# The low parts of split weights made by an adding DMA instead of vector subtractions

## The chip, the cores and the metric

The kernel runs on one core of one Trainium2 chip. The metric is device microseconds (us) of one execution; the median of several runs counts. The core has five engines with a queue each: TensorE (PE; PEld is its weight load), VectorE (DVE), ScalarE (ACT), GpSimd (POOL) and SyncE (SP, which issues transfers). All of them share 16 DMA engines.

## What is computed

Two layers of an encoder trunk over 512 positions of width 1024, all in float32. Each layer has a mixer (one input projection, a gated part, attention with 8 query and 2 key heads, one output projection) and a channel mixer (up projection, a convolution of width 3 over positions, gate, down projection).

```python
D_MODEL, SEQ, DEPTH, D_FF = 1024, 512, 2, 2816
for i in range(DEPTH):
    h = rms_norm(x, attn_norm_g[i])
    proj = h @ w_in[i]
    q, k, v, u, vv = jnp.split(proj, split_at, axis=-1)
    q = axial_rope(rms_norm(q, q_norm_g[i]), tables)
    k = axial_rope(rms_norm(k, k_norm_g[i]), tables)
    attn_o = gqa_attention(q, k, v)
    sg_o = spatial_gating(jax.nn.gelu(u), jax.nn.gelu(vv),
                          sg_norm_g[i], sg_w[i], sg_b[i])
    merged = jnp.concatenate([rms_norm(attn_o, attn_out_g[i]),
                              rms_norm(sg_o, sg_out_g[i])], axis=-1)
    x = x + merged @ w_o[i]
    h = rms_norm(x, ffn_norm_g[i]) @ w_up[i]
    h = depthwise_conv(h, conv_w[i], conv_b[i])
    gate, up = jnp.split(h, 2, axis=-1)
    x = x + (jax.nn.silu(gate) * up) @ w_down[i]
```

## The kernel before

Matmuls run on a rounded type (float32r). To keep accuracy each operand is split into a rounded high part and a low part, the difference; a product is three matmuls, high x high, high x low, low x high (`mm3`, L258).

All weights lie in memory as a list of 178 chunks of 128 x 1024 values (512 KB), in the order of use: per layer four chunks for vv, four for a1 (keys, values and the first half of the queries), four for u, two for a2 (the other queries), one for ws (the gating weights), four for so and four for ao (the output projection), and then 66 for the up and down projections (`up`, `dn`). The class `WStream` (L86) carries them: `load_to` issues a load from SP into one of 4 raw buffers (`wraw`), `split_to` makes the two parts in one of 6 split buffers (`wspl`, high part in `t[:, 0]`, low part in `t[:, 1]`). The high part is a rounding copy on ACT (L123). The low part is a subtraction, raw minus high (L125), on POOL for u, a2, so and ao (in two halves) and on DVE for all others. A raw buffer comes free when its low part is made, a split buffer when its last matmul has run. `next` (L134) is called where a chunk is used; it asks for loads six chunks ahead and for splits three ahead, and a scheduler then places each instruction in its engine's queue, so that the splits of a chunk stand further ahead where a buffer allows it.

One layer runs like this. `in_group("vv")` and `in_group("a1")` project; between them and beside them DVE makes the row scale r (`row_rsqrt`, `rsqrt`, L210: a chain of a dozen operations on 128 x 4 values), ACT and DVE the gelu and norm of vv (`vv_stat`, `vv_norm`; POOL multiplies vvg by the gain at L409), then the query and key statistics (`qk_stat`, ACT square at L326; `qk_norm`) and the rotation (`rope_pair`, L349 to L355, on DVE for K, on POOL for one pair of queries). At the start of each layer POOL makes the rotary tables (`tab`, L293, L297). A list written by hand, `PROG_AT`, sets the order of the rest of the mixer on TensorE: U are pieces of the u projection, K the transposes of the rotated K (L361), C scores, T transposes of P (L489), Z the output projection. In `up(j)` TensorE multiplies two chunks into two banks, and `up_post` does the convolution and gate on DVE and ACT (L669 to L683). `down(g)` uses pairs of chunks in the same way. DVE's L708 adds to x.

Of the kernel before, what the change touches and what calls it, by code (L numbers as in the profile page):

```python
# [10 lines left out]
F32 = mybir.dt.float32  # L11
F32R = mybir.dt.float32r
I32 = mybir.dt.int32
AF = mybir.ActivationFunctionType
ALU = mybir.AluOpType
# [70 lines left out]
class WStream:  # L86
# [25 lines left out]
    def split_to(self, n):  # L112
        nc = self.nc
        while self.split < min(n, len(PLAN)):
            i = self.split
            key, n_el = PLAN[i]
            raw = self.raw.pop(i)
            t = self.split_pool.tile([P, 2, CH], F32R, name="wspl")
            pieces = 2 if i == 0 or pool_lo(key) else 1
            st = n_el // pieces  # L120
            for a in range(0, n_el, st):
                e = slice(a, a + st)
                nc.scalar.activation(out=t[:, 0, e], in_=raw[:, e], func=AF.Copy)  # L123
                lo = nc.gpsimd if pool_lo(key) else nc.vector
                lo.tensor_tensor(out=t[:, 1, e], in0=raw[:, e], in1=t[:, 0, e].bitcast(F32), op=ALU.subtract)  # L125
            self.spl[i] = t
            self.split += 1
# [11 lines left out]
        return self.spl.pop(i)  # L139


def pool_lo(key):
    return key[0] in POOL_LO


ROPE_ENG = (0, 0)
WARM = 8
POOL_LO = ("u", "a2", "so", "ao")


@with_exitstack
# [661 lines left out]
```

## Time and profile before

| | |
|---|---|
| runs | 1126.06 us median of 3 (1125.95 to 1127.46) |
| span of the profiled execution | 1123.4 us; its own time is not listed apart from the span, which is 2.7 us under the median of the runs |
| mean granted TensorE clock | 0.989 |
| PE, DVE, ACT, POOL busy | 97%, 71%, 45%, 20% |
| DMA | 99.76 MB, 89 GB/s in the mean |

A row of the waits tells which engine and line waited, for which engine and line, how long in total, how often, and the longest. A timeline row tells the start, the duration, the engine, the line, the operation, output and inputs; idle time before it and what ended that stand in brackets. A window row tells how long each engine was busy in a stretch, the granted clock as a share of full speed, the DMA engines' busy share and GB/s.

### The profile page before, as it was taken

What the parts mean: (1) busy time and instruction counts of PE and PEld (TensorE: products, weight loads), DVE (VectorE), ACT (ScalarE), POOL (GpSimd) and SP (SyncE); (2) the same over time, 40 slices, a digit from 0 to 9 for tenths busy, and PEclk for the clock granted to TensorE, in tenths of its full rate; (3) what the DMA queues carried; (4) which work ended last, traced back from release to release, by engine and by line L of the source; (5) the groups of instructions that cost most, each with busy time, mean ns of one, the idle gap of its engine ahead of it and who ended that gap; (6) DMA issues with size and microseconds to landing.
All of it is one profiled execution on the core that took longest, in us unless ns stands there. A gap on an engine that the chain in (4) does not pass through costs nothing.

```text
span 1123.4 us, 13306 instructions
## 1 busy us (share of the span) xinstructions
PE 1085.4 (97%) x5024; PEld 903.1 (80%) x5024; DVE 801.9 (71%) x1210; ACT 502.2 (45%) x786; POOL 224.0 (20%) x221
## 2 busy tenths in 40 slices
PE   9969899999999999999999789999999999999998
PEld 7859687788888888888888688787888888888887
DVE  7898998787753777347668899977877447763573
ACT  6348683454431444224344586644444124441330
POOL 6665642200000000000166564421000000000000
PEclk9989999999999999999999899999999999999999
DMA  7321103232323323232332220122232322323201
GB/s 263 121 94 57 38 1 111 77 106 82 113 89 99 96 92 113 76 111 94 97 114 74 76 76 1 38 75 95 94 113 79 109 94 94 107 81 113 88 25 75
DMA packets 29439, 99.76 MB, mean 89 GB/s; under 512 B 3392, under 2 KB 4032, under 8 KB 29376
## 3 DMA queue, kind: packets, MB, share of 16 engines
q1 hardware_dynamic: 29088, 98.79, 26.3%
q8 instruction: 39, 0.64, 0.2%
q14 instruction: 24, 0.20, 0.1%
q10 hardware_dynamic: 288, 0.14, 0.0%
HBM read 96.82 MB, written 2.10 MB: 88 GB/s over the span
## 4 chain that ended last, share of the span: by engine, by line
PE 71%; DVE 7%; ACT 1%; issue 1%; POOL 1%; DVEq 0%; ACTq 0%
PE dn L261 7%; PE dn L260 7%; PE dn L259 7%; PE upg L260 7%; PE upg L261 7%; PE upv L261 7%; PE upv L259 7%; PE upv L260 7%; PE upg L259 7%; PE pT L489 1%; DVE wspl L125 1%; DVE xl L255 1%; PE vv L260 1%; PE vv L259 1%; PE vv L261 1%
## 5 line engine op out<-in xcount | busy, mean ns | idle before, releaser
L123 ACT ACTIVATE wspl<-wraw 128x1024 fp32r<-128x1024 f32 (+1 forms) x207 | 191.8, 938 | 249.9 <-PE dn L261 136.7
L125 DVE TENSOR_TENSOR wspl<-wraw,wspl 128x1024 fp32r<-128x1024 f32 (+1 forms) x151 | 191.4, 1269 | 92.7 <-ACT wspl L123 92.5
L259 PE MATMUL upg<-xh,wspl 128*128 128x512 f32 x352 | 137.4, 390 | 2.1 <-ACT xh L254 2.1
L260 PE MATMUL upg<-xl,wspl 128*128 128x512 f32 x352 | 137.2, 390 | 1.1 <-DVE xl L255 1.1
L261 PE MATMUL upv<-xh,wspl 128*128 128x512 f32 x352 | 137.0, 389 | 0.0
L260 PE MATMUL upv<-xl,wspl 128*128 128x512 f32 x352 | 137.0, 389 | 0.0
L261 PE MATMUL upg<-xh,wspl 128*128 128x512 f32 x352 | 137.0, 389 | 0.0
L259 PE MATMUL upv<-xh,wspl 128*128 128x512 f32 x352 | 136.9, 389 | 0.0
L259 PE MATMUL dn<-g,wspl 128*128 128x512 f32 x352 | 136.9, 389 | 0.0
L260 PE MATMUL dn<-g,wspl 128*128 128x512 f32 x352 | 136.9, 389 | 0.0
L261 PE MATMUL dn<-g,wspl 128*128 128x512 f32 x352 | 136.9, 389 | 0.0
L671 ACT ACTIVATE ht<-ht,pk_sb 128x512 f32<-128x512 f32 x88 | 70.9, 808 | 69.0 <-DVE ht L669 69.0
L708 DVE TENSOR_TENSOR x<-x,dn 128x512 f32<-128x512 f32 x63 | 43.0, 685 | 66.3 <-PE dn L261 66.2
L672 DVE SCALAR_TENSOR_TENSOR ht<-ht,pk_sb 128x511 f32<-128x511 f32 x88 | 65.7, 747 | 33.0 <-ACT ht L671 33.0
L125 POOL TENSOR_TENSOR wspl<-wraw,wspl 128x512 fp32r<-128x512 f32 x56 | 77.6, 1408 | 49.8 <-ACT wspl L123 49.8
L259 PEld LDWEIGHTS upg<-xh,wspl 128*128 128x128 f32 x352 | 66.1, 188 | 16.5 <-ACT xh L254 2.9
L260 PEld LDWEIGHTS upg<-xl,wspl 128*128 128x128 f32 x352 | 66.1, 188 | 15.6 <-DVE xl L255 2.1
L682 ACT ACTIVATE g<-ht 128x512 fp32r<-128x512 f32 x44 | 27.7, 631 | 110.8 <-DVE ht L678 110.8
L261 PEld LDWEIGHTS upv<-xh,wspl 128*128 128x128 f32 x352 | 66.1, 188 | 13.8
L259 PEld LDWEIGHTS upv<-xh,wspl 128*128 128x128 f32 x352 | 66.1, 188 | 13.7
L259 PEld LDWEIGHTS dn<-g,wspl 128*128 128x128 f32 x352 | 66.1, 188 | 13.7
L260 PEld LDWEIGHTS dn<-g,wspl 128*128 128x128 f32 x352 | 66.1, 188 | 13.7
(198 smaller groups left out, 2049.5 us busy)
## 6 DMA issues: line engine op xcount, KB each, us to landing
wraw<-in_wts SPq DMA_DIRECT2D x177, 512.0 KB, 3.4
x<-in_xT SPq DMA_DIRECT2D x8, 256.0 KB, 6.0
out_y<-x SPq DMA_DIRECT2D x7, 256.0 KB, 2.0
wraw<-in_wts SPq DMA_DIRECT2D x2, 256.0 KB, 3.9
sgn<-in_gq SPq DMA_DIRECT2D x2, 256.0 KB, 4.7
rope<-in_rope SPq DMA_DIRECT2D x2, 256.0 KB, 4.9
pk_sb<-in_pk SPq DMA_DIRECT2D x1, 208.0 KB, 7.2
gq_sb<-in_gq SPq DMA_DIRECT2D x2, 64.0 KB, 5.1
```

The lines of the kernel that those rows point to most:

```text
L123: nc.scalar.activation(out=t[:, 0, e], in_=raw[:, e], func=AF.Copy)
L125: lo.tensor_tensor(out=t[:, 1, e], in0=raw[:, e], in1=t[:, 0, e].bitcast(F32), op=ALU.subtract)
L255: V.scalar_tensor_tensor(out=lo, in0=x_sb[d], scalar=gcol, in1=hi.bitcast(F32), op0=ALU.mult, op1=ALU.subtract)
L259: T.matmul(out, lhsT=lh, rhs=rh, start=start, stop=False)
L260: T.matmul(out, lhsT=lh, rhs=rl, start=False, stop=False)
L261: T.matmul(out, lhsT=ll, rhs=rh, start=False, stop=stop)
L489: T.transpose(bank[:, b * P:(b + 1) * P], pt[b][:, s * P:(s + 1) * P], ident)
L671: A.activation(out=tt, in_=h, func=AF.Identity, scale=col(PK_CW + 2 * NCT + ct), bias=col(PK_CB + ct))
L672: V.scalar_tensor_tensor(out=tt[:, 1:S], in0=h[:, 0:S - 1], scalar=col(PK_CW + ct), in1=tt[:, 1:S], op0=ALU.mult, op1=ALU.add)
L682: A.activation(out=hi, in_=t[0], func=AF.Copy)
L708: V.tensor_tensor(out=x_sb[dt], in0=x_sb[dt], in1=bank, op=ALU.add)
```

## The change

The low part of every chunk but those of vv is made in three steps: ACT writes the high part, ACT writes the negated high part into the place of the low part, and a DMA issued from POOL adds the raw chunk onto it. The vv chunks keep the subtraction on DVE. The halves on POOL go with the subtractions there, so all chunks but the first are split in one piece. There are 170 such DMAs of 512 KB each, and 170 more copies on ACT; 142 subtractions leave DVE and 56 (halves) leave POOL. One line is added above the rest, so the line numbers after it are higher by one.

```diff
-            pieces = 2 if i == 0 or pool_lo(key) else 1
+            pieces = 2 if i == 0 else 1
             st = n_el // pieces
             for a in range(0, n_el, st):
                 e = slice(a, a + st)
                 nc.scalar.activation(out=t[:, 0, e], in_=raw[:, e], func=AF.Copy)
-                lo = nc.gpsimd if pool_lo(key) else nc.vector
+                if key[0] in DMA_LO:
+                    nc.scalar.activation(out=t[:, 1, e], in_=raw[:, e], func=AF.Copy, scale=-1.0)
+                    nc.gpsimd.dma_start(out=t[:, 1, e].bitcast(F32), in_=raw[:, e], accum_op=ALU.add)
+                    continue
+                lo = nc.gpsimd if key[0] in POOL_LO else nc.vector
                 lo.tensor_tensor(out=t[:, 1, e], in0=raw[:, e], in1=t[:, 0, e].bitcast(F32), op=ALU.subtract)
...
-def pool_lo(key):
-    return key[0] in POOL_LO
...
-POOL_LO = ("u", "a2", "so", "ao")
+POOL_LO = ()
+DMA_LO = ("a1", "u", "a2", "ws", "so", "ao", "up", "dn")
```

POOL's queue in the first layer, from the last sums of squares to the vvg products and the rotation of a pair of queries. Before:

```order
L226 TENSOR_TENSOR sqacc<-sqacc,sq 128x512 x2
L293 TENSOR_TENSOR tab<-rope,gq_sb 128x256
L297 TENSOR_TENSOR tab<-rope,gq_sb 128x4x16 x4
L293 TENSOR_TENSOR tab<-rope,gq_sb 128x256
L297 TENSOR_TENSOR tab<-rope,gq_sb 128x4x16 x4
L125 TENSOR_TENSOR wspl<-wraw,wspl 128x512 x6
L409 TENSOR_TENSOR vvg<-vvg,sgn 128x512 x2
L125 TENSOR_TENSOR wspl<-wraw,wspl 128x512
L409 TENSOR_TENSOR vvg<-vvg,sgn 128x512 x2
L125 TENSOR_TENSOR wspl<-wraw,wspl 128x512 x5
L349 TENSOR_TENSOR rot<-qn,tab 128x512
```

The same place of POOL's queue now:

```order
L227 TENSOR_TENSOR sqacc<-sqacc,sq 128x512 x2
L126 DMA wspl<-wraw 128x1024
L294 TENSOR_TENSOR tab<-rope,gq_sb 128x256
L298 TENSOR_TENSOR tab<-rope,gq_sb 128x4x16 x4
L294 TENSOR_TENSOR tab<-rope,gq_sb 128x256
L298 TENSOR_TENSOR tab<-rope,gq_sb 128x4x16 x4
L126 DMA wspl<-wraw 128x1024 x6
L410 TENSOR_TENSOR vvg<-vvg,sgn 128x512 x4
L126 DMA wspl<-wraw 128x1024 x3
L350 TENSOR_TENSOR rot<-qn,tab 128x512
```

The first a1 chunk's low part is issued ahead of the tables; those of the three other a1 chunks and of the first three u chunks stand between the tables and vvg; the four vvg products now stand together.

ACT's queue in the steady part of the up projection, one block of `up` (L671 and L672 are the convolution's middle tap, L677 and L678 the silu, L682 and L683 the rounded gate product). Before:

```order
L671 ACTIVATE ht<-ht,pk_sb 128x512
L123 ACTIVATE wspl<-wraw 128x1024
L677 ACTIVATE ht<-ht 128x512
L123 ACTIVATE wspl<-wraw 128x1024
L671 ACTIVATE ht<-ht,pk_sb 128x512
L682 ACTIVATE g<-ht 128x512
```

The same block of ACT's queue now, where L123 is the rounded and L125 the negated copy:

```order
L672 ACTIVATE ht<-ht,pk_sb 128x512
L123 ACTIVATE wspl<-wraw 128x1024
L678 ACTIVATE ht<-ht 128x512
L125 ACTIVATE wspl<-wraw 128x1024
L123 ACTIVATE wspl<-wraw 128x1024
L672 ACTIVATE ht<-ht,pk_sb 128x512
L125 ACTIVATE wspl<-wraw 128x1024
L683 ACTIVATE g<-ht 128x512
```

The rounded copies stand where they stood; each negated copy follows one instruction later.

## Rows read from the trace of the kernel before

**Rows 1.** The page, part 1: busy us (share of the span) and instructions.

```profile
PE 1085.4 (97%) x5024; PEld 903.1 (80%) x5024; DVE 801.9 (71%) x1210; ACT 502.2 (45%) x786; POOL 224.0 (20%) x221
```

**Rows 2.** Waits of PE and PEld over the span.

```profile
PE tr L361 <- DVE rot L355: 17.1, 2, 9.4
PE pT L489 <- DVE att L505: 4.9, 2, 2.5
PE ps L231 <- DVE asq L524: 4.1, 2, 2.0
PE pT L489 <- ACT p L470: 2.7, 2, 1.4
...
PEld pT L489 <- POOL wspl L125: 3.5, 2, 1.8
```

**Rows 3.** Windows: each engine's busy us (instructions), granted clock, DMA share, GB/s.

```profile
300.00:350.00 50.00, 50.00 (x223) 41.38 (x222) 25.94 (x30) 14.96 (x17) 0.00 (x0) 1.00 0.30 96
...
8.00:12.00 4.00, 4.00 (x13) 3.12 (x13) 3.08 (x4) 4.00 (x7) 2.65 (x2) 1.00 1.03 407
...
72.00:76.00 4.00, 1.58 (x6) 1.51 (x7) 4.00 (x7) 0.46 (x1) 3.40 (x2) 0.50 0.00 0
...
628.00:632.00 4.00, 3.96 (x13) 3.30 (x14) 4.00 (x6) 1.11 (x2) 2.67 (x2) 0.51 0.05 5
```

**Rows 4.** Timeline of ACT in the up projection: a split and its wait.

```profile
299.82 1.06 ACT L123 ACTIVATE wspl<-wraw 128x1024 fp32r<-128x1024 f32 x1 [0.82 <-PE upv L261]
```

**Rows 5.** The page, part 5: groups, busy us, mean ns of one, idle before.

```profile
L123 ACT ACTIVATE wspl<-wraw 128x1024 fp32r<-128x1024 f32 (+1 forms) x207 | 191.8, 938 | 249.9 <-PE dn L261 136.7
L125 DVE TENSOR_TENSOR wspl<-wraw,wspl 128x1024 fp32r<-128x1024 f32 (+1 forms) x151 | 191.4, 1269 | 92.7 <-ACT wspl L123 92.5
...
L125 POOL TENSOR_TENSOR wspl<-wraw,wspl 128x512 fp32r<-128x512 f32 x56 | 77.6, 1408 | 49.8 <-ACT wspl L123 49.8
```

**Rows 6.** Load queue from 240 to 560 us (packets, MB, share); loads, ns; landing.

```profile
q1 hardware_dynamic: 8643, 31.01, 29.4%
...
L108 SPq DMA_DIRECT2D wraw<-in_wts x177: 327/328/665, 3.5 to 1067.8; - x177
...
DMA to landing us min/median/max: 3.1/3.4/7.4
```

**Rows 7.** Timelines of DVE and POOL in the first layer, and DVE in the second.

```profile
31.25 1.17 DVE L214 TENSOR_SCALAR rxr<-rxt 128x4 int32<-128x4 int32 x1
...
36.60 0.16 DVE L218 SCALAR_TENSOR_TENSOR rxr<-rxa,rxr 128x4 f32<-128x4 f32 x1
...
61.31 1.21 DVE L332 TENSOR_SCALAR qass<-qass 128x24 f32<-128x24 f32 x1
...
29.99 1.15 POOL L297 TENSOR_TENSOR tab<-rope,gq_sb 128x64 f32<-128x64 f32 x4
31.10 5.05 POOL L125 TENSOR_TENSOR wspl<-wraw,wspl 128x512 fp32r<-128x512 f32 x4
...
48.12 3.37 POOL L409 TENSOR_TENSOR vvg<-vvg,sgn 128x512 f32<-128x512 f32 x2 [3.10 <-DVE vvg L407]
...
587.53 1.21 DVE L214 TENSOR_SCALAR rxr<-rxt 128x4 int32<-128x4 int32 x1
```

**Rows 8.** Timelines of ACT and PE around the query statistics and the K wait.

```profile
58.19 1.61 ACT L326 ACTIVATE sq<-a 128x384 f32<-128x384 f32 x4
...
612.39 1.61 ACT L326 ACTIVATE sq<-a 128x384 f32<-128x384 f32 x4
...
30.68 0.49 PE L259 MATMUL a<-wspl,xh 128*128 128x512 f32 x1
...
52.58 0.39 PE L259 MATMUL u<-wspl,xh 128*128 128x512 f32 x1
...
607.93 0.39 PE L259 MATMUL u<-wspl,xh 128*128 128x512 f32 x1
...
76.16 0.63 PE L261 MATMUL u<-wspl,xl 128*128 128x512 f32 x1
76.59 0.63 PE L259 MATMUL u<-wspl,xh 128*128 128x512 f32 x1
```

## The prediction

> **What bounds the kernel now.** I read the busy shares first, then the waits of TensorE, then windows. PE is busy 1085.4 of 1123.4 us [rows 1]; whatever the change does elsewhere, it can give back at most the 38 us in which PE stands still, plus what a lowered clock costs, and it can take much more than that by making PE wait for weights. The waits of PE [rows 2] say where those 38 us lie: 17.1 us are two waits (one in each layer) of the K transposes for the rotated K, 4.9 + 2.7 us are waits of the P transposes, 4.1 us the wait for asq. None of any size is for a weight chunk. The windows [rows 3] add two things. From 300 to 350 us, in the up and down projections, PE has no gap at all: 223 matmuls in 50 us, 0.224 us each, so a chunk of 1024 columns (24 matmuls) lasts 5.4 us. And right after the K waits the granted clock stands near 0.5 (0.50 and 0.51, the 1.2 GHz level) before it returns to 1.00. So the kernel has two kinds of stage: a long one (2 x 66 chunks) where weights must come every 5.4 us and nothing can be gained, and the mixer of each layer, where VectorE's chain to K is what PE waits for.
>
> **Up and down projections: the DMA engines.** Here the change must not make weights late. Two numbers decide: how early a chunk is split, and whether the 16 DMA engines can carry it. For the first, the splits of ScalarE [rows 4] wait for the end of a matmul that frees one of six split buffers, so the new chunk is wanted six chunks after the one that was just used up: five lie between, 5 x 5.4 = 27 us, less 2.7 us because the two chunks of a pair are used in alternation. That leaves 24 us. Before, the split took 1.06 + 1.27 us [rows 5]. Now it takes 1.06 for the rounded part, 1.06 for the negated part, an issue on POOL and a transfer. ScalarE's order keeps the rounded part at the same place in each block, the negated one one step later. No row shows a DMA issued from POOL. Its issue lies between 0.33 us (SP's issue of the same 512 KB) and 2.8 us (the two POOL subtractions of a chunk that go away, 1.4 us each) [rows 5, 6]; I take 1 us, nearer to the SP row as both only issue. Landing takes 3.1 us at the least for a plain chunk, 7.4 at the most [rows 6]; with twice the reading I take 6 to 10. Sum 2.1 + 1 + 10 = 13 of 24 us: hidden. A raw buffer, of which there are four, is now held until the transfer lands: load 3.4 to 7.4, split 2.1, issue 1, transfer 6 to 10, so 13 to 20 us of the 4 x 5.4 = 21.7 that four buffers give. Hidden too, with little left at the upper end. ScalarE's added 170 x 1.06 = 180 us lie in its idle time: it is busy 502 us (45%) [rows 1] and goes to about 61%. VectorE loses 142 subtractions of 1.27 us, 180 us, all of it cover for nothing: worth zero in this stage.
>
> For the second: from 240 to 560 us the load queue takes 29.4% of the engines while 59 chunks land [rows 6], so one load costs 0.294 x 320 / 59 = 1.6 us of all 16 engines. An add reads 512 KB twice and writes it once. At the least it costs as much as one load, 1.6 us; the rows give no upper end, so I set it at four loads, 6.4 us, as an assumption. I take two loads, 3.2 us, since the 8:12 window [rows 3] shows the engines moving 407 GB/s when pushed (two readings of 512 KB at that rate are 2.6 us, just under it). Then a chunk needs 1.6 + 3.2 = 4.8 of 5.4 us: 88% busy, but not the bound. This term is zero, and it is the thinnest one: it holds up to 2.4 loads per add.
>
> The Trainium skill speaks to both sides. "Collectives: The Full Stack", section "The bandwidth ceiling", says that an add inside a DMA costs no time of its own but two source reads, which halves the rate; by it the add would be two loads, the same 4.8 us. "DMA: Bandwidth & Descriptors", section "Issuing engines are not separate DMA queues", speaks against the change: transfers issued from POOL share the 16 engines with those from SP, so the added 89 MB are not free. No row here shows either.
>
> **The mixer: what VectorE gains.** In the first layer VectorE's tiny operations take 1.2 us instead of 0.16 while POOL subtracts [rows 7]: four in the chain of r (31.25 to 36.2), two at 43, three from 60.7 to 63.8. Together 4.1 + 1.8 + 2.4 = 8.3 us. The second layer shows the same at the same places, 6.7 us over seven operations, one of the first 1.21 [rows 7]. These POOL subtractions go: 14 chunks per layer, two halves each. Not all of this reaches K. The square of the query projection on ScalarE (58.19, behind a split and the vh copies, which wait for POOL) could start when a1 ends on PE at 52.6; in the second layer 612.39 against 607.9 [rows 8]. So the ceiling is 5.5 + 2.4 = 7.9 of the 9.4 us wait, and 4.5 + 1.9 = 6.4 of the 7.7.
>
> What works against it in the first layer: the low part of a1's second chunk is now issued on POOL behind the rotary tables, which end at 31.1 [rows 7] and a little later now, because the first chunk's issue stands ahead of them. Ready at 32.2 + 1 + 3.4 to 7 = 36.6 to 40.2; PE wants it at 30.7 + 5.4 = 36.1. That stall of 0.5 to 4 us moves the end of a1 with it. On POOL the vvg products of the first layer also stand behind six such issues, the last of which waits for a load that waits for an earlier low part; by my count vvg starts at 48.5 instead of 48.1 [rows 7], but then runs without a subtraction in between. I take 4.5 us for the first layer (0 to 7.9) and 5.5 for the second (2 to 6.4), where the tables are not in the way.
>
> The clock: after the K waits the matmuls start 0.43 us apart [rows 8] instead of 0.224 for some ten instructions, about 2.3 us in each layer. With a wait of 2 to 4 us left it may fall or not; I take half, 2.5 of 4.6 us. The P transposes: 3.5 us of weight loads there wait behind a POOL subtraction [rows 2], and the chain of the second query group runs beside four more. Of 7.6 us of PE waits I take 2 back (0 to 5). Against all that stand some four extra 1.06 us copies per layer on ScalarE while it is nearly full with the softmax: 1 us (0 to 5). In the output projection and at the start of up the low parts leave VectorE and go behind POOL's sums of squares; they are wanted at least 10 us later, so zero.
>
> Whether a DMA issue on POOL holds VectorE as a subtraction does is in no row. "SBUF — State Buffer", section "Who interferes with whom", gives the hold to a VectorE operation with two SBUF inputs beside a POOL instruction that reads SBUF; an issue only writes descriptors, and by it the sum stands. If it held VectorE all the same, this part would be zero.
>
> **Sum.** 4.5 + 5.5 + 2.5 + 2 - 1 = 13.5 us off the span of 1123.4, so 1109.9. The median of the runs, 1126.06, is 2.7 us above the span; carried over, 1112.6: I say 1113, with 1101 (all ceilings: 7.9 + 6.4 + 4.6 + 5 = 24) to 1122 for this case.
>
> **Rivals.**
> *The DMA engines become the bound* (slower). Place: both projections, 132 chunks. Point: an add of more than 2.4 loads (3.8 us). Price: (1.6 + add - 5.4) x 132, less the 13 won elsewhere. At 2.7 loads 5.9 us a chunk, +63, about 1170; at three loads 6.4 us, +127, about 1240; at four, +340, about 1450. For it: adds mean read, read, write through engines that are 29% busy already, and no row bounds the add. Against: 407 GB/s in the start window.
> *POOL's queue turns the mixer around* (slower). 19 issues per layer take the place of 28 subtractions of 1.4 us; at more than 2 us an issue, POOL is busier than before, and vvg, the rotary products and the softmax scaling stand behind issues that wait for ScalarE. At 4 us an issue I count 10 to 20 us lost over both layers: 1128 to 1146.
> *Nothing moves* (no change): the end of a1 and of vvg are held by late low parts, or an issue holds VectorE as the subtraction did. The K waits stay: 1122 to 1129.
> That the subtractions stay where they were can be left out; the program has 170 such DMAs and nine subtractions of vv.
>
> **How the numbers follow.** Forecast 0.55, DMA engines 0.24, POOL's queue 0.10, nothing 0.11. About 0.2% (2.3 us) is what a measurement can tell from no change. Faster: 0.55 and a little of the last, 0.57. Same: 0.09. Slower: 0.34. For 8 in 10 the range runs from 1101 to 1170: above it lies about two thirds of the DMA case, 0.16, and below it 0.03.
>
> **What would show it.** Right: PE without gaps from 250 to 550, DMA share there near 0.9 and landing of the adds under 10 us, VectorE's tiny operations at 0.16 to 0.19 us outside POOL's own products, the K waits down to 2 to 5 us. Wrong: TensorE waiting for wspl by a DMA in the up and down projections with the DMA share at 1, POOL's queue full, or K waits as long as before with vvg later.

## The result, and the profile after

The changed kernel takes 1096.37 us (median of 4 runs, 1094.58 to 1098.38) against 1126.57 us (1125.95 to 1127.46) for the kernel before beside it: a ratio of 0.972, 95% interval 0.9694 to 0.9746. It is 30 us faster where 13 were forecast, and 5 us below the range of 1101 to 1170. The profiled execution of after has a span of 1095.3 us and took 1097.05 us; the span was 1123.4 before, so the traces have 28.1 of the 30 us to explain. Line numbers of after are one higher than before from the split on; L125 is now the negated copy, L126 the adding DMA, and L129 the subtraction of vv.

The page of after, busy us of each engine, then the group of the adding DMA's issues (x count | busy us, mean ns | idle before, releaser):

```profile
PE 1079.0 (99%) x5024; PEld 898.0 (82%) x5024; DVE 597.2 (55%) x1068; ACT 656.9 (60%) x928; POOL 280.0 (26%) x335
...
L126 POOL DMA_DIRECT2D wspl<-wraw x170 | 147.3, 868 | 666.9 <-ACT wspl L125 381.9
```

Against [rows 1], VectorE has lost 205 us of work and ScalarE has gained 155. Neither number is the gain. PE's standing time went from 38.0 to 16.3 us, and that is where 22 of the 28 us are; the other 6 are PE's own busy time (1085.4 to 1079.0), which is shorter where the granted clock no longer falls (4.5 us by the table and the windows below; what made up the rest is open).

The waits of PE in after (us in total, times, longest), to hold against [rows 2]:

```profile
PE tr L362 <- DVE rot L356: 5.8, 2, 5.1
PE pT L490 <- ACT p L471: 1.9, 2, 1.0
PE a L260 <- ACT p L471: 1.4, 2, 0.7
```

The K wait fell from 17.1 to 5.8 us, nearly all of it in the first layer. The wait of the P transposes for att (4.9 us), the wait for asq (4.1 us) and the weight loads behind a POOL subtraction (3.5 us) are no longer in the list. One wait is new: the a2 matmuls (tile a) for ScalarE's p, 0.7 us in each layer.

**Where the 28 us lie.** The same instruction of TensorE in both traces, by its start (us from the start of the span), gives the lead of after at ten points. Of matmuls in three products the first product is taken:

| instruction of PE | before | after | lead | gained since the row above |
|---|---|---|---|---|
| first K transpose, layer 1 | 74.42 | 70.39 | 4.0 | 4.0 |
| first so matmul, layer 1 | 129.7 | 123.8 | 5.9 | 1.9, P transposes |
| first ao matmul, layer 1 | 175.9 | 167.6 | 8.2 | 2.3, output projection |
| first dn matmul, layer 1 | 313.2 | 302.9 | 10.4 | 2.1, start of up |
| first vv matmul, layer 2 | 563.46 | 553.10 | 10.4 | 0.0, up and down |
| first K transpose, layer 2 | 628.04 | 610.70 | 17.3 | 7.0, K |
| last u matmul, layer 2 | 640.2 | 621.0 | 19.2 | 1.8, clock after K |
| last P transpose, layer 2 | 715.2 | 693.0 | 22.2 | 3.0, P transposes |
| last ao matmul, layer 2 | 756.3 | 730.2 | 26.1 | 3.9, output projection |
| last dn matmul, layer 2 | 1118.9 | 1090.7 | 28.2 | 2.2, start of up |

The two long flat stretches (no change from 313 to 563 us, nor in the last 330 us) say that the projections gave and took nothing. All of it is in the mixers and at the seam to up.

The second layer gained more than the first in the P transposes and the output projection, and the clock is why. Before, the granted clock stood at 0.50 behind the wait for att and behind the wait for asq of that layer, and did not fall behind the same waits of the first (1.00 from 122 to 126 and from 172 to 176 us). Windows of before in those stretches:

```profile
676.30:679.70 3.40, 3.40 (x19) 3.40 (x18) 3.34 (x7) 2.70 (x6) 3.12 (x6) 0.50 0.00 0
727.50:730.90 3.40, 3.40 (x10) 2.72 (x10) 2.35 (x14) 0.00 (x0) 0.00 (x0) 0.50 0.24 96
```

In after the clock is 1.00 over the same matmuls. The lead grows by 1.0 and 1.6 us in these stretches; with the 1.8 after K the clock gave back 4.5 us.

**The projections.** Windows of after (busy us and instructions of each engine, granted clock, DMA share, GB/s): the up projection, the stretch of vv and a1 in the first layer, and the matmuls after its K wait; in the second fence, from 240 to 540 us, the two queues and the issues (KB each, median us to landing):

```profile
300.00:350.00 50.00, 50.00 (x222) 41.41 (x221) 9.79 (x14) 21.95 (x23) 8.60 (x10) 1.00 0.81 196
20.00:64.00 44.00, 44.00 (x199) 36.53 (x198) 24.18 (x62) 27.65 (x39) 20.19 (x26) 1.00 0.96 235
72.00:76.00 4.00, 4.00 (x15) 3.18 (x15) 1.88 (x3) 2.75 (x5) 0.86 (x1) 0.67 0.69 135
```

```profile
q0 software_dynamic: 7744, 28.18, 52.7%
q1 hardware_dynamic: 8208, 29.43, 27.8%
...
wraw<-in_wts SPq DMA_DIRECT2D x56, 512.0 KB, 4.2
wspl<-wraw POOLq DMA_DIRECT2D x53, 512.0 KB, 4.9
```

In up, PE has no gap (50.00 of 50.00), as in [rows 3], while the DMA share went from 0.30 to 0.81. One add costs 0.527 x 300 / 53 = 2.98 us of all 16 engines and one load 0.278 x 300 / 56 = 1.49 us: the add is two loads, as the prediction took it (3.2 and 1.6 us). The Trainium skill, "Collectives: The Full Stack", section "The bandwidth ceiling", has two source reads for an add, which halves the rate; this trace agrees, with 2.98 against 1.49 us. In 20 to 64 us the share is 0.96: ten loads and ten adds are issued in these 44 us, one of each every 4.4 us, against one load every 5.4 us in up. That second row matters below.

**The holds.** Before, POOL's subtraction of an so chunk and VectorE's multiplication of att by pk ran at the same time, and at the start of up VectorE did a subtraction between x and xl. Timelines of before (start, us, engine, line, operation):

```profile
164.54 5.26 DVE L513 SCALAR_TENSOR_TENSOR ats<-att,pk_sb,ats 128x512 fp32r<-128x512 f32 x3
...
164.51 6.42 POOL L125 TENSOR_TENSOR wspl<-wraw,wspl 128x512 fp32r<-128x512 f32 x4 [5.26 <-ACT wspl L123]
...
210.71 1.21 DVE L125 TENSOR_TENSOR wspl<-wraw,wspl 128x1024 fp32r<-128x1024 f32 x1
```

Timelines of after: the multiplication, the operation at L333 (L332 in [rows 7]), and an operation of K's chain with the issue of a DMA on POOL beside it:

```profile
158.56 1.40 DVE L514 SCALAR_TENSOR_TENSOR ats<-att,pk_sb,ats 128x512 fp32r<-128x512 f32 x2
...
59.06 0.18 DVE L333 TENSOR_SCALAR qass<-qass 128x24 f32<-128x24 f32 x1
...
60.35 0.18 DVE L217 TENSOR_TENSOR qaa<-qaf 128x24 f32<-128x24 f32 x1
...
60.17 0.85 POOL L126 DMA_DIRECT2D wspl<-wraw  x1 [2.55 <-ACT wspl L125]
```

Three multiplications in 5.26 us became 0.7 us each; the sum of att behind them, and with it asq's last sum, came early with them. The operation at L333 takes 0.18 us where [rows 7] had 1.21; it has one input, so operations with one input were held too. And the row at 60.35 us settles what no row of before could: an issue on POOL does not hold VectorE, since the operation inside its 0.85 us took 0.18 us. The Trainium skill, "SBUF — State Buffer", section "Who interferes with whom", names the hold for a VectorE operation with two SBUF inputs beside a POOL instruction that reads SBUF; the trace agrees: three such multiplications took 5.26 us with a POOL subtraction beside them and take 0.7 us each without.

### The profile page after: what moved, and what is told of

Same layout as the page of the kernel before. It is cut to its first block, busy times and chain, and to the rows that moved or that the text cites. A ratio compares the mean times of both kernels' runs of the same rounds, so it can differ in the third digit from the quotient of the medians.

```text
span 1095.3 us, 13699 instructions
## 1 busy us (share of the span) xinstructions
PE 1079.0 (99%) x5024; PEld 898.0 (82%) x5024; DVE 597.2 (55%) x1068; ACT 656.9 (60%) x928; POOL 280.0 (26%) x335
## 4 chain that ended last, share of the span: by engine, by line
PE 89%; DVE 4%; DMA 3%; ACT 1%; POOL 1%; issue 1%; SPq 0%; DVEq 0%; ACTq 0%; POOLq 0%
PE upg L260 7%; PE upv L261 7%; PE upg L262 7%; PE upg L261 7%; PE upv L262 7%; PE dn L262 7%; PE dn L260 7%; PE upv L260 7%; PE dn L261 7%; DMA wraw<-in_wts 2%; PE pT L490 2%; PE so L260 1%; PE so L262 1%; PE ao L261 1%; PE so L261 1%; PE ao L262 1%
## 5 line engine op out<-in xcount | busy, mean ns | idle before, releaser
L126 POOL DMA_DIRECT2D wspl<-wraw x170 | 147.3, 868 | 666.9 <-ACT wspl L125 381.9
L123 ACT ACTIVATE wspl<-wraw 128x1024 fp32r<-128x1024 f32 (+1 forms) x179 | 188.5, 1053 | 201.9 <-PE dn L262 57.4
L125 ACT ACTIVATE wspl<-wraw 128x1024 fp32r<-128x1024 f32 x170 | 177.8, 1046 | 0.0
L672 ACT ACTIVATE ht<-ht,pk_sb 128x512 f32<-128x512 f32 x88 | 70.6, 807 | 67.8 <-DVE ht L670 67.8
L670 DVE TENSOR_TENSOR ht<-upv,rb 128x512 f32<-128x512 f32 x44 | 30.4, 690 | 87.5 <-PE upv L262 87.2
L262 PEld LDWEIGHTS dn<-g,wspl 128*128 128x128 f32 x352 | 66.1, 188 | 13.7
L260 PEld LDWEIGHTS dn<-g,wspl 128*128 128x128 f32 x352 | 66.1, 188 | 13.7
L261 PEld LDWEIGHTS dn<-g,wspl 128*128 128x128 f32 x352 | 66.1, 188 | 13.7
```

The costliest lines, as they stand in the source:

```text
L125: nc.scalar.activation(out=t[:, 1, e], in_=raw[:, e], func=AF.Copy, scale=-1.0)
L126: nc.gpsimd.dma_start(out=t[:, 1, e].bitcast(F32), in_=raw[:, e], accum_op=ALU.add)
L260: T.matmul(out, lhsT=lh, rhs=rh, start=start, stop=False)
L261: T.matmul(out, lhsT=lh, rhs=rl, start=False, stop=False)
L262: T.matmul(out, lhsT=ll, rhs=rh, start=False, stop=stop)
L670: V.tensor_tensor(out=h, in0=banks[i], in1=rb[0], op=ALU.mult)
```

## The experiments

Theory H: the gain is POOL's subtractions gone, because each held VectorE's operations beside it (in K's chain, in the P transposes, before asq). Theory V: the gain is VectorE's own 142 subtractions gone, which stood in its queue. All kernels of this section are the changed kernel with the edit shown, or the kernel before with single kinds of chunks given to the DMA. Kinds of chunks in neither list of an edit are subtracted on VectorE, those in POOL_LO in two halves on POOL, as before. Lines of the waits are: us in total, times, longest.

**1. Only the kinds that POOL subtracted before.**

```diff
-DMA_LO = ("a1", "u", "a2", "ws", "so", "ao", "up", "dn")
+DMA_LO = ("u", "a2", "so", "ao")
```

> Only the chunks that POOL subtracted before (u, a2, so, ao) take their low part from the adding DMA; a1, ws, up and dn are subtracted on VectorE as before. Theory H (POOL's subtractions held VectorE's operations): the ends of K, of the P transposes and of asq come early as after the change (12.9 + 4.9 + 6.1 us of lead), only the 4.2 us at the start of up stay: 30 - 4 = 26 us, about 1100. Theory V (VectorE was loaded with its own subtractions): these are all still there, so 0 to 8 us, 1118 to 1126.

Measured: 1096.32 us, ratio 0.9728 (0.9699 to 0.9757), the same as the whole change, although VectorE is busy 769.6 us (597.2 in after). As the main cause theory V is out; what is left of it is the start of up (run 5). Waits of PE:

```profile
PE upg L260 <- ACT xh L255: 2.1, 2, 1.0
PE tr L362 <- DVE rot L356: 1.3, 2, 0.8
PE upg L261 <- DVE xl L256: 1.1, 2, 0.6
```

The waits at the start of up stayed (3.2 us), as H has it. But the K wait is 1.3 us, not the 5.8 of after: taking a1 and ws off the DMA gained another 4.5 us. So the full change pays something back in the first layer, which runs 10 to 12 follow.

**2. The mirror image: only the kinds that VectorE subtracted before.**

```diff
+POOL_LO = ("u", "a2", "so", "ao")
+DMA_LO = ("a1", "ws", "up", "dn")
```

> The mirror image: a1, ws, up and dn by the adding DMA, while u, a2, so and ao stay two half subtractions on POOL. Theory H: only the start of up gains, 4 us, about 1122, and VectorE's 128x4 operations still take 1.2 us beside POOL. Theory V: most of the 30 us, 1097 to 1105.

Measured: 1124.52 us, ratio 0.9966 (0.9954 to 0.9979). VectorE is relieved here (628.7 us busy) and almost nothing is won. Waits of PE, and two groups of VectorE (x count | busy us, mean ns):

```profile
PE tr L362 <- DVE rot L356: 20.4, 2, 11.2
PE pT L490 <- DVE att L506: 4.9, 2, 2.5
PE ps L232 <- DVE asq L525: 4.1, 2, 2.1
```

```profile
L514 DVE SCALAR_TENSOR_TENSOR ats<-att,pk_sb,ats 128x512 fp32r<-128x512 f32 x8 | 12.0, 1538 | 0.0
L333 DVE TENSOR_SCALAR qass<-qass 128x24 f32<-128x24 f32 x2 | 2.4, 1204 | 0.1
```

The three waits of [rows 2] are all here, the K wait even 3.3 us longer, and the held operations still take 1.2 and 1.5 us.

**3. No adding DMA at all, and nothing subtracted on POOL.**

```diff
-DMA_LO = ("a1", "u", "a2", "ws", "so", "ao", "up", "dn")
+DMA_LO = ()
```

> No adding DMA at all: every low part is one subtraction on VectorE, none on POOL. Theory H: the holds are gone (23.9 us of lead), against them 14 further subtractions of 1.27 us per layer stand in VectorE's order between the mixer's own operations, 18 us per layer of which perhaps half lies in a chain: net 0 to 15 us, 1111 to 1126. Theory V: VectorE is loaded more than before, so slower, 1130 to 1145.

Measured: 1112.34 us, ratio 0.9857 (0.984 to 0.9874): 16 us faster with no DMA added and 28 subtractions more on VectorE, which is nevertheless busy 795.8 us, less than the 801.9 of [rows 1]: what the held operations lose is more than the new ones take. Moving a subtraction off POOL helps even when it goes onto the engine whose chain TensorE waits for. What it does not win is VectorE's own time for them. Waits of PE:

```profile
PE tr L362 <- DVE rot L356: 10.5, 2, 5.4
PE pT L490 <- ACT p L471: 4.9, 2, 2.5
```

**4. Only so and ao.**

```diff
+POOL_LO = ("u", "a2")
+DMA_LO = ("so", "ao")
```

> Of the mixer's chunks only so and ao (the output projection) go to the adding DMA, u and a2 stay on POOL, the rest on VectorE as before. Theory H: the multiply of att by pk takes 0.7 instead of 5.26 us, asq comes early, 6.1 us over both layers and perhaps part of the P transposes: 1116 to 1120; the waits for K stay near 9.4 and 7.7 us. Theory V: nothing, 1126.

Measured: 1117.57 us, ratio 0.9912 (0.9882 to 0.9942), 11 us faster, as theory H has it. The profiled run is the longest of five (1122.54 us, mean granted clock 0.985), so its trace is read for the waits and the holds, not for the 11 us. Waits of PE and the held group:

```profile
PE tr L362 <- DVE rot L356: 17.3, 2, 9.6
PE pT L490 <- ACT p L471: 1.9, 2, 0.9
```

```profile
L514 DVE SCALAR_TENSOR_TENSOR ats<-att,pk_sb,ats 128x512 fp32r<-128x512 f32 x8 | 5.8, 745 | 0.1
```

The waits for att and for asq are gone, the K wait stands untouched. So the so and ao chunks carry the P transposes and the output projection (4.9 + 6.2 = 11.1 us of the table), and u and a2 carry most of K. For the P transposes, rows of before around the wait for att that ends at 121.79 us:

```profile
112.04 5.15 POOL L125 TENSOR_TENSOR wspl<-wraw,wspl 128x512 fp32r<-128x512 f32 x4
117.17 1.36 POOL L472 TENSOR_SCALAR p<-p,sm 128x512 f32<-128x512 f32 x2
...
115.25 0.72 DVE L213 TENSOR_SCALAR qbt<-qbss 128x16 int32<-128x16 int32 x1
...
121.06 0.67 DVE L505 TENSOR_TENSOR att<-att,pv 64x512 f32<-64x512 f32 x1
```

Two things happen here. VectorE's statistics of the second query group are held (0.72 us at L213, where the undisturbed operations of this size take 0.17), and the att sum that the transposes wait for stands behind them. And POOL's own scaling of p (L472), which the transposes read, stands behind four halves. The products of vvg on POOL show the same: the third starts at 53.15 us, behind a half of 1.73 us. Every run that takes subtractions from POOL frees its queue and VectorE together. That the subtractions on POOL cost the time is shown by runs 1 to 4; how much of it by the holds and how much by POOL's own order was not separated. Theory H names the holds alone, and to that extent it is argued from the rows, not shown by a run.

**5. Only up and down.**

```diff
+POOL_LO = ("u", "a2", "so", "ao")
+DMA_LO = ("up", "dn")
```

> Only the up and down chunks by the adding DMA, everything in the mixer as before. If the sum of the places is right, the start of up gains its 4.2 us (VectorE's four subtractions of 1.21 us between x and xl are gone) and nothing else: about 1122. If the adds in up and down also help the mixer through VectorE, more: 1110 or less. If they cost anything by the DMA engines: 1126 or more.

Measured: 1123.52 us, ratio 0.9951 (0.9931 to 0.997), 5.2 us faster: the start of up, where the waits for xh and xl (3.2 us) are gone from PE's list. The other waits of [rows 2] are all still there (17.3, 4.9 and 4.0 us).

**6 and 7. How much the DMA engines have left: a further quarter or half chunk added.** For each up or down chunk a further add onto a scratch tile; K2_BUFS 24 instead of 25 for its room. There are 132 such chunks in both layers together.

```diff
+                    if key[0] in ("up", "dn"):
+                        for j in range(1):   # 2 in the second
+                            nc.gpsimd.dma_start(out=self.scr[j], in_=raw[:, 256 * j:256 * j + 256], accum_op=ALU.add)
```

> The changed kernel, and behind each of the 132 x 2 adds of the up and down chunks a further add of a quarter chunk (128 x 256) onto a scratch tile that nobody reads; K2_BUFS is 24 instead of 25 to make room. If an add costs 2.98 us of the 16 engines for 512 KB (from the engines' share in 240 to 540 us), load + add + quarter are 1.6 + 3.0 + 0.75 = 5.35 us of the 5.44 us that a chunk lasts on TensorE: still hidden, 1097 to 1105. If the engines' share understates what an add costs, TensorE waits for weights: 1110 or more.

> The same with two quarter adds (half a chunk more): 1.6 + 3.0 + 1.5 = 6.1 us against 5.44 us, 0.65 us over on each chunk: times 264 chunks in both layers +170 us, or times 132 +86 us if a chunk lasts longer than that; TensorE waits for wspl, DMA share near 1. If it stays near 1097 the engines carry more than their shares say.

Measured: 1255.19 us (ratio 1.1116) and 1331.67 us (1.1794), far from both expectations; and the DMA share in 300 to 350 us was 0.82 and 0.86, so the engines were not full. Two waits of POOL in the first of the two, and rows of ScalarE and POOL, say why:

```profile
POOL scr L129 <- DMA wraw<-in_wts: 463.1, 62, 10.2
POOL scr L129 <- DMA scr<-wraw: 125.4, 57, 3.6
```

```profile
296.03 1.04 ACT L125 ACTIVATE wspl<-wraw 128x1024 fp32r<-128x1024 f32 x1
...
309.72 0.87 POOL L129 DMA_DIRECT2D scr<-wraw  x1 [8.38 <-DMA wraw<-in_wts]
312.67 0.86 POOL L129 DMA_DIRECT2D scr<-wraw  x1 [2.09 <-PE upv L268]
313.21 2.10 POOL L126 DMA_DIRECT2D wspl<-wraw  x2
```

An add onto the scratch tile needs only the raw chunk, so in POOL's order it came to stand a pair of chunks early, ahead of the adds of the pair before. POOL stood up to 10 us at an issue that waited for a load, with adds queued behind it that were ready: the first add at 313.21 us is of the chunk whose negated copy ended at 297.07. Those adds held the raw buffers that the next loads needed. A second, smaller wait is for the scratch tile itself, which every chunk writes again. The two runs measured the order on POOL's queue, not what the engines can carry.

**8 and 9. The same bytes, issued with their own chunk.** The extra add reads the rounded part of the same chunk, so its issue waits for that copy. The edit is that of the quarter, with two scratch tiles in turn; the half has two such adds for each chunk, one onto each tile. K2_BUFS is 24 again. The extra add now also keeps the split buffer busy instead of the raw one.

```diff
+                    if key[0] in ("up", "dn"):
+                        nc.gpsimd.dma_start(out=self.scr[i % 2], in_=t[:, 0, 0:256].bitcast(F32), accum_op=ALU.add)
```

> The extra quarter add again (128 x 256 onto a scratch tile that nobody reads), but its source is the rounded part of the same chunk, so that POOL issues it right behind that chunk's own add and no issue waits for a later load. Theory B (the 16 engines' share tells what an add costs, 2.98 us for 512 KB): 1.6 + 3.0 + 0.75 = 5.35 of 5.44 us a chunk, still hidden, 1097 to 1105; the 158 us of the first quarter run were then the order on POOL's queue. Theory C (the engines carry less than their shares say): 1.2 us more on each of 132 chunks, again about 1255.

> Two such quarter adds behind each add of an up or down chunk. Theory B: 1.6 + 3.0 + 1.5 = 6.1 us of engines against 5.44 us of TensorE, 0.65 us over on 132 chunks, +86 us, about 1183, with TensorE waiting for wspl and a DMA share of 0.95 or more. Theory C: 1.78 us a chunk as in the first half run, about 1330.

Measured: 1099.25 us (ratio 0.9745, 0.9709 to 0.978) and 1157.05 us (1.0257, 1.0222 to 1.0293). For the quarter, a window in the up projection and two rows of POOL:

```profile
350.00:400.00 50.00, 50.00 (x222) 41.44 (x221) 25.65 (x36) 30.55 (x37) 14.94 (x18) 1.00 0.96 218
```

```profile
354.74 0.86 POOL L128 DMA_DIRECT2D scr<-wspl  x1 [6.35 <-ACT wspl L123]
356.21 0.86 POOL L126 DMA_DIRECT2D wspl<-wraw  x1 [0.61 <-PE upv L267]
```

POOL issues the extra add just ahead of the same chunk's own add, which is ready at 355.92 us and goes out 0.3 us later. The engines stand at 0.96 to 0.99 from 300 to 500 us and PE has not one gap. Theory B holds here, and the same quarter of a chunk that cost 159 us in run 6 costs 3 us, less than the two runs differ (1097.14 and 1101.36).

For the half, a window, the wait of PE for adds of up, and rows of ScalarE and POOL:

```profile
450.00:500.00 50.00, 46.79 (x202) 37.26 (x201) 13.59 (x20) 20.07 (x22) 22.57 (x26) 1.00 1.05 223
```

```profile
PE upg L268 <- DMA wspl<-wraw: 13.9, 16, 3.3
```

```profile
347.72 1.04 ACT L125 ACTIVATE wspl<-wraw 128x1024 fp32r<-128x1024 f32 x1
352.82 1.06 ACT L123 ACTIVATE wspl<-wraw 128x1024 fp32r<-128x1024 f32 x1 [4.06 <-DMA wraw<-in_wts]
...
353.91 1.75 POOL L129 DMA_DIRECT2D scr<-wspl  x2 [3.42 <-ACT wspl L123]
354.98 1.56 POOL L126 DMA_DIRECT2D wspl<-wraw  x1
```

The share passes 1 and PE waits, as theory B has it. But the order on POOL's queue is at fault again: the add at 354.98 us is of the chunk whose negated copy ended at 348.76, and it stood behind a scratch add that waited for the rounded copy of the next chunk, which waited for its load. So run 9 does not settle what the engines can carry. From 240 to 540 us a chunk lasted 300 / 50 = 6.0 us, and the half cost 61 us over after where 86 were expected; how much of that is the engines and how much the order is not shown. One side of the rival's edge is shown: load, add and quarter, 5.35 us a chunk by the expected sum, do not bind.

**10. a1 and ws alone back on VectorE.**

```diff
-DMA_LO = ("a1", "u", "a2", "ws", "so", "ao", "up", "dn")
+DMA_LO = ("u", "a2", "so", "ao", "up", "dn")
```

> The changed kernel with a1 and ws alone taken back to VectorE. If the K wait left in the first layer (5.1 us, and the clock that falls behind it) comes from a1's part of the DMA traffic, it goes: 1096.4 - 4 to 6 = about 1091. If it comes from ScalarE's added copies of all kinds, it stays: 1095 to 1098.

Measured: 1090.39 us, ratio 0.9667 (0.9645 to 0.9688), 6 us faster than the whole change. ScalarE's timeline in after before the query statistics (sq), then what after's loads waited for from 30 to 60 us, and then the same instruction sq and the DMA share of vv and a1 in this run:

```profile
54.46 1.06 ACT L123 ACTIVATE wspl<-wraw 128x1024 fp32r<-128x1024 f32 x1 [1.40 <-DMA wraw<-in_wts]
56.37 1.61 ACT L327 ACTIVATE sq<-a 128x384 f32<-128x384 f32 x4
```

```profile
SPq L108 <- DMA wspl<-wraw: 28.2, 7, 5.7
```

```profile
51.87 1.61 ACT L327 ACTIVATE sq<-a 128x384 f32<-128x384 f32 x4
```

```profile
20.00:64.00 44.00, 44.00 (x199) 36.54 (x198) 36.41 (x76) 24.81 (x36) 27.67 (x28) 1.00 0.81 208
```

In after, ScalarE waits for a raw chunk before a split that stands ahead of sq; with a1 and ws on VectorE sq starts 4.5 us earlier, and the engines are at 0.81 instead of 0.96 there. The raw chunk was late because its buffer was: the load for the split at 54.46 us was issued at 47.18, when an add issued at 36.95 had landed, 10 us later. The clock stays at 1.00 after K in this run; in after it fell, and its mean from 72 to 76 us was 0.67. So the 5.1 us of K wait left in the first layer were a price of giving a1 and ws to the DMA. Fuller engines, raw buffers held until an add lands, and more copies on ScalarE all go with these chunks, and this run takes them away together.

**11. The best of both: u, a2, so, ao and up by the DMA.**

```diff
-DMA_LO = ("a1", "u", "a2", "ws", "so", "ao", "up", "dn")
+DMA_LO = ("u", "a2", "so", "ao", "up")
```

> u, a2, so, ao and up by the adding DMA; a1, ws and dn subtracted on VectorE as before. The run with only u, a2, so, ao had no K wait left (1.3 instead of 5.8 us) but kept the start of up. If both gains add, 1096.4 - 4.2 to 4.5 = about 1092 and the waits of TensorE there for xh and xl go; if the adds of up press on the DMA engines in the next stage, 1096 or more.

Measured: 1089.94 us, ratio 0.9664 (0.9645 to 0.9683): both gains add, within 2 us of the figure given. With run 10 it is the fastest kernel of this study; the two cannot be told apart, so the adds of down bring nothing and cost nothing.

**12. Three raw buffers.**

```diff
-RAW_BUFS, SPL_BUFS, K8_BUFS, K2_BUFS = 4, 6, 8, 25
+RAW_BUFS, SPL_BUFS, K8_BUFS, K2_BUFS = 3, 6, 8, 25
```

> The changed kernel with three raw buffers instead of four. A raw buffer is held for load 4.3 + wait and split 2.1 + issue 0.9 + add 5.0 = 12.3 us; three give 3 x 5.44 = 16.3 us. If that sum is right, up and down stay without a gap on TensorE and the time stays within 5 us of 1096; the prediction's upper end (20 us) would not fit and TensorE would wait for wspl there, 3.7 us on every third chunk or +160 us.

Measured: 1105.7 us, ratio 0.978 (0.9746 to 0.9814), 9 us slower than the whole change, twice the bound given. The projections did as expected: PE is busy 50.00 of 50.00 us in each of four windows between 250 and 500 us, so a raw buffer is held for less than 16.3 us. The miss is in the mixer, the stage that the sum left out, where loads and adds come faster than one in 5.4 us:

```profile
PE tr L362 <- DVE rot L356: 10.6, 2, 8.5
```

```profile
20.00:64.00 44.00, 44.00 (x200) 36.51 (x199) 23.41 (x59) 25.23 (x34) 19.39 (x25) 1.00 0.93 223
```

The K wait grew from 5.8 to 10.6 us, 8.5 of it in the first layer. That is the same weakness as in run 10, loads that come late between 20 and 64 us, and here with the engines at 0.93, not fuller than in after. It speaks for the held buffers as at least part of the cause.

## Why the prediction was wrong, point by point

**Bound and stages: right, but for the start of up.** PE's standing time in the mixers, with the clock behind it, was most of the prize, and 300 to 350 us neither gained nor lost. The seam between mixer and up, 4.3 us, was counted to the stage in which nothing can be gained.

**Up and down, zero: right, with its sizes.** The add was put at two loads and measured 2.98 against 1.49 us; the share forecast as 0.88 is 0.81; landing was forecast at 6 to 10 us and is 4.9 us (median) there; the issue was taken as 1 us and took 0.87. The rival of the DMA engines did not come; run 8 shows room for a quarter of an add more, and no run shows cleanly where the room ends. Two small slips of the working change nothing: by its own price 2.7 loads an add give 1176 us, not 1170, and 24 us off the median are 1102, not 1101.

**K and the clock: right in sum, in part by luck.** Forecast 4.5 + 5.5 + 2.5 = 12.5 us; measured 4.0 + 7.0 + 1.8 = 12.8. The second layer gained more than its ceiling of 6.4. In the first layer the 4.0 us are what a larger gain left: with a1 and ws on VectorE (runs 1, 10 and 11) K came 8.6 to 9.1 us early, over the ceiling of 7.9, and the a1 chunks on the DMA took half of that back. The feared stall of a1's second chunk did not come (a1 started 0.3 us later), but what followed was of the same kind, a raw chunk that came late. The clock came back in the second layer alone, as the wait of the first stayed at 5.1 us, and it gave back 2.6 us more behind the waits for att and asq, for which the prediction had no term. Runs 1, 2 and 3 show that it was mostly POOL's subtractions that made the K wait.

**P transposes less ScalarE's copies: mis-sized.** Forecast 2 - 1 = 1 us; measured 4.9. Of 7.6 us of waits 5.7 went (4.9 to 0, 2.7 to 1.9), and the clock gave 1.0. Against that stands a cost of 1.9 us where 1 was forecast: the new wait of the a2 matmuls for ScalarE's p, at which the lead falls by 0.9 us in each layer. It stands in runs 1, 4, 10, 11 and 12 too, in which the so chunks get the negated copy, and not in runs 2, 3 and 5, in which they do not; that the copy makes it is argued from this alone.

**The failing step: "In the output projection and at the start of up the low parts leave VectorE and go behind POOL's sums of squares; they are wanted at least 10 us later, so zero."** Measured 2.3 + 3.9 us in the output projection and 2.1 + 2.2 us at the start of up, 10.5 us together (1.6 of them clock), of the 14.6 by which the sum of 13.5 missed the 28.1 in the spans. The step asked only when the low part is wanted, which was right: it is wanted late. It did not ask what the subtraction held up while it ran, and it took all these low parts for VectorE's, though those of so and ao were made on POOL. On VectorE that is the queue: among the last operations on x, xh and xl of each layer stood subtractions of 1.21 us, three of them from 202 to 212 us in the first layer, and each put the operation behind it and with it the next matmuls back (run 5 shows the gain). On POOL it is the hold: three multiplications that need 0.7 us each took 5.26 us beside four halves, and the att sum behind them started at 169.83 us instead of about 166.6 (164.54 + 3 x 0.7; run 4 shows the hold gone). The wait for asq of 4.1 us in [rows 2], read as one of three places in the first part of the prediction, got no term of the sum at all.

That step (10.5 us against 0) and the P transposes (4.9 against 1) are nearly the whole miss of 14.6 us. The upper end of the prediction's own case, 24 us, was short for the same reason: its ceilings were those of the places it had priced.

**Rivals.** POOL's queue as the bound did not come: an issue takes 0.87 us and two halves took 2.8. But run 6 shows its mechanism at full size when one issue waits for a load. "Nothing moves" fell with the row at 60.35 us, which shows that an issue holds nothing on VectorE.

## What to carry to other kernels

When work leaves an engine, list what ran beside it and what was queued behind it in every stage, and price those; when its own result is wanted is the smaller question. Every wait that was found in the view of waits should have a term in the sum, if only zero with its reason. And a DMA that is issued by an engine with other work keeps its place in that engine's order: an issue that waits for data must not stand ahead of one that is ready.

## What the runs showed of the hardware

- An adding DMA from one SBUF tile onto another costs the 16 engines twice a load of the same 512 KB, 2.98 against 1.49 us, and lands in 4.9 us (7.5 us in 20 to 60 us, at a share of 0.95).
- Load and adds kept the engines at a share of 0.96 to 0.99 from 300 to 500 us (run 8) without a gap on TensorE. Such shares are sums of packet times and can pass 1 (1.05 in run 9).
- The issue of such a DMA on POOL takes 0.87 us and does not hold VectorE's small operations (0.18 us inside it); a subtraction on POOL does (1.21 us), those with one input too.
- A subtraction on POOL is dearer to this kernel than one on VectorE: with all of them on VectorE the kernel is 16 us faster than with 56 halves on POOL (run 3).
- The same added bytes cost 3 or 159 us over after's time (1099 against 1255 us for a quarter) by their source, which sets what their issues wait for on POOL's queue; it also sets which buffer the add holds, and the runs do not part the two.
